# A decoder layer on one core: the down projection as seven products of halves, with the sums of weights made by adding DMAs

## The chip, the core and the metric

The kernel runs on one core of a Trainium2 chip. The metric is the device time of one execution in microseconds (us). TensorE is called PE here (its weight loads PEld), VectorE DVE, ScalarE ACT, GpSimd POOL, and the SyncE queue that issues most DMAs SP.

## What is computed

One layer of a decoder for 512 tokens of width 1024, in float32: token mixers, an output projection, a gated feed-forward part with a causal convolution of width 3, and a last RMS norm. What matters here is the end of it:

```python
x  = x + merged @ w_out[l]                       # (512, 1024)
def conv_gated_ffn(h, w_up, conv_w, conv_b, w_down):
    up = causal_depthwise_conv(h @ w_up, conv_w, conv_b)     # (512, 5632)
    gate, val = jnp.split(up, 2, axis=-1)
    return (jax.nn.silu(gate) * val) @ w_down                # (512, 2816) @ (2816, 1024)
x  = x + conv_gated_ffn(rms_norm(x, ffn_norm[l]), ...)
return rms_norm(x, final_norm)
```

## The kernel before

Everything is float32, and TensorE multiplies a rounded form of it (F32R). To keep the precision each operand is split in two: a cast on ACT gives the high part, a subtraction on DVE the low part (`wsplit` for weights, L65; `split` for activations, L75), and each product is three matmuls, high with high, high with low and low with high (`mm3`, L79). So a weight tile goes through a DMA on SP's queue (`wtile`, three buffers of 128x1024), an ACT cast (L70, three buffers), a DVE subtraction (L71, three buffers) and then PE. The order of the instructions on each engine is drawn up by a scheduler when the program is built: it goes by the order of the program, but lets an instruction pass earlier ones that are not ready yet by its own estimate of times. On the chip each engine then follows its list in order.

The last three stages are those around the change:

- Output projection (L561 to L581): the residual stream x1 is held with features on the partitions, 8 tiles of 128 features x 512 tokens.
- Up stage (L615 to L627): 22 pairs of up projections (gate and value), each 8 x 3 matmuls of 512 columns into one PSUM bank (`up`, L591), then the convolution on DVE and ACT (`conv`, L600), SiLU, the product with the value and a split into aH[i] and aL[i] (L627): 22 blocks of 128 features x 512 tokens.
- Down stage (L642 to L736): out = w_down^T a, features on the partitions. Six blocks of 128 output features take 22 x 3 matmuls of 512 columns each (tiles pd, L648). The last 256 features go by 384 tokens in two banks (pA, L690) and, for the last 128 tokens, with tokens on the partitions (pB, L706), so that the norm of these is short. For that, x1 of the last tokens is transposed on PE in the middle (L694), means are taken on PE (L695, L712) and spread (L714).

The tail is everything behind the last matmul: a square with its sum on ACT (L727), two small steps on DVE and POOL for the inverse root (L729, L731), the scaling (L732 to L734) and two output DMAs (L735, L736).

## Time and profile before

| | |
|---|---|
| median of 3 runs | 707.83 us (707.31 to 708.87) |
| the profiled execution's own time | 707.67 us |
| its span on the core | 705.8 us |
| PE busy | 698.0 us (99%) |
| DVE busy | 476.1 us (67%) |
| ACT busy | 332.4 us (47%) |
| POOL busy | 12.3 us (2%) |
| DMA | 69.63 MB, mean 99 GB/s |

Busy time is that of one execution. Matmuls are pipelined: a row's duration (389 ns for 512 columns) is longer than the distance from one start to the next, and it is the distance that counts. The profiled execution lies 0.16 us under the median.

### The profile page before, as it was taken

How to read it: one execution, taken by the hardware profiler on the slowest of the kernel's cores; microseconds unless marked ns; L12 is line 12 of the kernel's file. 1: busy time of each engine (PE TensorE's matmuls, PEld its weight loads, DVE VectorE, ACT ScalarE, POOL GpSimd, SP SyncE). 2: the span in 40 equal slices, each digit the busy share in tenths (PEclk: the TensorE clock that was granted, in tenths of full speed). 3: DMA queues.
4: the chain of work that ended last, by engine and by line, in shares of the span. 5: the costliest groups of instructions: out<-in, count | busy, mean ns of one | idle time of the engine just before them, and what ended most of it. 6: DMA issues, size and time to landing. Idle time of an engine off the chain costs nothing.

```text
span 705.8 us, 8631 instructions
## 1 busy us (share of the span) xinstructions
PE 698.0 (99%) x3303; PEld 587.1 (83%) x3303; DVE 476.1 (67%) x817; ACT 332.4 (47%) x497; POOL 12.3 (2%) x16
## 2 busy tenths in 40 slices
PE   9999999999999999999999999999999999999996
PEld 6888888888888888888888888888888888888896
DVE  7976799877777578755587777777777775433104
ACT  5465566676667533433464444444444444423101
POOL 0000110000000000000100000000000000000000
PEclk9999999999999999999999999999999999999998
DMA  8524422131211122533222232223222335631003
GB/s 255 184 71 143 168 83 82 60 113 47 70 64 61 39 81 80 188 99 111 90 90 91 92 115 91 91 92 115 92 90 91 104 90 164 193 89 47 0 1 120
DMA packets 22617, 69.63 MB, mean 99 GB/s; under 512 B 2736, under 2 KB 4400, under 8 KB 22576
## 3 DMA queue, kind: packets, MB, share of 16 engines
q1 hardware_dynamic: 21568, 66.72, 29.0%
q10 hardware_dynamic: 1008, 2.36, 0.9%
q8 instruction: 26, 0.43, 0.2%
q14 instruction: 15, 0.12, 0.1%
HBM read 66.97 MB, written 2.10 MB: 98 GB/s over the span
## 4 chain that ended last, share of the span: by engine, by line
PE 97%; DMA 1%; DVE 1%; SPq 0%; issue 0%; POOLq 0%; ACT 0%; DVEq 0%
PE pup L82 11%; PE pup L81 11%; PE pup L80 11%; PE pd L81 4%; PE pd L82 4%; PE pd L80 4%; PE pout L81 2%; PE pv L80 2%; PE pout L80 2%; PE pza L80 2%; PE pzb L80 2%; PE pza L81 2%; PE pzu L81 2%; PE pzb L82 2%; PE pzb L81 2%; PE pza L82 2%
## 5 line engine op out<-in xcount | busy, mean ns | idle before, releaser
L70 ACT CAST wh_u<-wr_u 128x1024 fp32r<-128x1024 f32 x44 | 46.3, 1052 | 41.3 <-PE pup L81 29.5
L71 DVE TENSOR_TENSOR wl_u<-wr_u,wh_u 128x1024 fp32r<-128x1024 f32 x44 | 53.9, 1226 | 8.0 <-ACT wh_u L70 7.0
L605 DVE TENSOR_TENSOR z<-pup,r 128x512 f32<-128x512 f32 x44 | 30.2, 688 | 35.2 <-PE pup L82 35.2
L80 PE MATMUL pd<-aH,wh_d 128*128 128x512 f32 x132 | 51.3, 389 | 0.0
L81 PE MATMUL pd<-aL,wh_d 128*128 128x512 f32 x132 | 51.3, 389 | 0.0
L82 PE MATMUL pd<-aH,wl_d 128*128 128x512 f32 x132 | 51.3, 389 | 0.0
L70 ACT CAST wh_g<-wr_g 128x1024 fp32r<-128x1024 f32 x24 | 25.2, 1049 | 46.2 <-issue 27.4
L76 ACT CAST aH<-y 128x512 fp32r<-128x512 f32 x22 | 13.7, 621 | 56.8 <-DVE z L604 54.2
L71 DVE TENSOR_TENSOR wl_d<-wr_d,wh_d 128x896 fp32r<-128x896 f32 (+1 forms) x18 | 20.5, 1136 | 29.0 <-ACT wh_d L70 27.6
L70 ACT CAST wh_d<-wr_d 128x896 fp32r<-128x896 f32 (+1 forms) x18 | 17.7, 982 | 43.0 <-PE pd L81 35.4
L607 ACT ACTIVATE y<-z,part 128x512 f32<-128x512 f32 x44 | 35.9, 818 | 3.1 <-DVE z L605 1.8
L71 DVE TENSOR_TENSOR wl_g<-wr_g,wh_g 128x1024 fp32r<-128x1024 f32 x24 | 29.4, 1223 | 7.0 <-ACT wh_g L70 6.9
L611 DVE SCALAR_TENSOR_TENSOR y<-z,part,y 128x512 f32<-128x512 f32 x44 | 33.0, 751 | 1.4
L609 DVE SCALAR_TENSOR_TENSOR y<-z,part,y 128x512 f32<-128x512 f32 x44 | 32.8, 747 | 0.3 <-ACT y L607 0.3
L624 ACT ACTIVATE y<-y 128x512 f32<-128x512 f32 x22 | 13.9, 632 | 36.6 <-DVE y L611 36.6
L80 PEld LDWEIGHTS pd<-aH,wh_d 128*128 128x128 f32 x132 | 24.8, 188 | 5.2
L81 PEld LDWEIGHTS pd<-aL,wh_d 128*128 128x128 f32 x132 | 24.8, 188 | 5.1
L82 PEld LDWEIGHTS pd<-aH,wl_d 128*128 128x128 f32 x132 | 24.8, 188 | 5.1
L81 PE MATMUL pout<-mL,wh_o 128*128 128x512 f32 x64 | 25.3, 395 | 0.0
L80 PE MATMUL pout<-mH,wh_o 128*128 128x512 f32 x64 | 25.0, 394 | 0.0
L82 PE MATMUL pout<-mH,wl_o 128*128 128x512 f32 x64 | 24.9, 389 | 0.0
L77 DVE TENSOR_TENSOR aL<-y,aH 128x512 fp32r<-128x512 f32 x22 | 15.2, 693 | 14.2 <-ACT aH L76 14.2
(595 smaller groups left out, 2004.8 us busy)
## 6 DMA issues: line engine op xcount, KB each, us to landing
wr_u<-in_w_u_dram SPq DMA_DIRECT2D x44, 512.0 KB, 3.3
wr_g<-in_w_g_dram SPq DMA_DIRECT2D x24, 512.0 KB, 3.3
wr_d<-in_w_d_dram SPq DMA_DIRECT2D x12, 448.0 KB, 3.5
x<-in_xT_dram SPq DMA_DIRECT2D x16, 256.0 KB, 4.2
wr_v<-in_w_v_dram SPq DMA_DIRECT2D x8, 512.0 KB, 4.3
wr_o<-in_w_o_dram SPq DMA_DIRECT2D x8, 512.0 KB, 3.3
wr_d<-in_w_d_dram SPq DMA_DIRECT2D x6, 512.0 KB, 3.5
wr_e<-in_w_e_dram SPq DMA_DIRECT2D x5, 512.0 KB, 3.8
```

Of the source, the lines that this page charges most:

```text
L70: A.copy(th[:, lo:hi], raw[:, lo:hi])
L71: V.tensor_tensor(out=tl[:, lo:hi], in0=raw[:, lo:hi], in1=th[:, lo:hi].bitcast(F32), op=ALU.subtract)
L76: A.copy(th, src)
L77: V.tensor_tensor(out=tl, in0=src, in1=th.bitcast(F32), op=ALU.subtract)
L80: T.matmul(o, lhsT=wh, rhs=xh, start=start, stop=False)
L81: T.matmul(o, lhsT=wh, rhs=xl, start=False, stop=False)
L82: T.matmul(o, lhsT=wl, rhs=xh, start=False, stop=stop)
L605: V.tensor_tensor(out=z[:, 2:], in0=pz, in1=r2, op=ALU.mult)
L607: A.activation(out=y, in_=z[:, 2:], func=AF.Identity, scale=part[:, w + 2:w + 3], bias=part[:, PCB + f:PCB + f + 1])
L609: V.scalar_tensor_tensor(out=y, in0=z[:, 1:S + 1], scalar=part[:, w + 1:w + 2], in1=y, op0=ALU.mult, op1=ALU.add)
L611: V.scalar_tensor_tensor(out=y, in0=z[:, 0:S], scalar=part[:, w:w + 1], in1=y, op0=ALU.mult, op1=ALU.add)
L624: A.activation(out=yg, in_=yg, func=AF.Silu)
```

## The change

The down projection is computed with tokens on the partitions, as a product of 2 x 2 halves: the tokens (A1, A2) and the 2816 inner features in halves on one side, the inner features and the 1024 output features in halves (B11, B12, B21, B22) on the other. Seven products of halves, m1, m5, m6, m4, m3, m7 and m2 in this order, take the place of eight. Each is 256 tokens x 1408 x 512 features: 11 inner blocks x 2 blocks of tokens x 3 matmuls of 512 columns, in six steps (two inner blocks each, one in the last) with one weight tile per step.

- The activations' sides: `up` no longer splits its result, but writes it to aT; every fourth pair `a_sides` makes the sums and differences of halves on DVE, and splits that of m1. The sides of the other six are split in the down stage (`a_split`, three blocks of up to 128x1024 per product, two steps ahead).
- The weights' sides: six tiles R hold B11, loaded on SP's queue in the up stage (pairs 12 to 17). After a tile has been split for one product (`w_split`, two steps ahead), the next half is added into it by a DMA from GpSimd's queue with an adding form (`fill` with `accum_op`): B12 after m1, B22 after m5, B21 after m6, B12 after m3, 24 adding DMAs in all. After m4, B22 is loaded plainly on SP's queue; m2 loads B21 through the tiles wr.
- The residual x1 is turned to tokens on the partitions in the up stage (`x1_turn`, eight times four PE transposes and one ACT copy), and added on DVE. The results of the products are added into it on DVE as they come (`post`); the norm is taken per token (`done`, `finish`), and each block of 128 tokens leaves by one DMA on SP's queue and one on ACT's.
- The last product runs its last three steps for one block of tokens and then for the other.
- gfb, the final gain on all partitions, is loaded on ACT's queue at the start of the down stage instead of on SP's at the start of the kernel. The layouts of w_u, w_d and the output follow; w_e is gone.

```diff
@@ -161,8 +160,8 @@
     hL = [None] * KC
 
     def htiles(j, n):
-        hH[j] = hp.tile([P, S], F32R, tag=f"hH{j}", name=f"hH{j}{n}")
-        hL[j] = hp.tile([P, S], F32R, tag=f"hL{j}", name=f"hL{j}{n}")
+        t = hp.tile([P, D], F32R, tag=f"h{j}", name=f"h{j}{n}")
+        hH[j], hL[j] = t[:, :S], t[:, S:]
...
-    vA = [hp.tile([P, D], F32, tag=f"d{t}", name=f"vA{t}") for t in range(NT)]
+    vA2 = [hp.tile([P, 2 * D], F32, tag=f"d{t}", name=f"vA{t}") for t in range(2)]
+    vA = [vA2[t // 2][:, (t % 2) * D:(t % 2 + 1) * D] for t in range(NT)]
...
-        SY.dma_start(gfb, fnl.to_broadcast([P, 2 * P]))
...
-        x1t = [hp.tile([P, D], F32, tag=f"d{t}", name=f"x1_{t}") for t in range(NT)]
-        x1 = [x1t[j // 2][:, (j % 2) * S:(j % 2 + 1) * S] for j in range(KC)]
+        x1t = [hp.tile([P, NT, NT, P], F32, tag=f"d{t}", name=f"x1_{t}") for t in range(2)]
+        x1 = [x1t[j // NT][:, j % NT].rearrange("p t c -> p (t c)") for j in range(KC)]
...
-    f2 = ctx.enter_context(tc.tile_pool(name="f2", bufs=2))
     r2 = fp.tile([P, S], F32, name="r2")
-    aH = [fp.tile([P, S], F32R, name=f"aH{i}") for i in range(NF)]
-    aL = [fp.tile([P, S], F32R, name=f"aL{i}") for i in range(NF)]
+    aT = fp.tile([P, NF, S], F32, name="aT")
+    KH = NF // 2
+    S2 = S // 2
+    s1 = fp.tile([P, KH, S2], F32, name="s1")
+    s4 = fp.tile([P, KH, S2], F32, name="s4")
+    a1h = fp.tile([P, KH, S2], F32R, name="a1h")
+    a1l = fp.tile([P, KH, S2], F32R, name="a1l")
+    steps = [(g, min(g + 2, KH)) for g in range(0, KH, 2)]
+    NS = len(steps)
+    B11, B12, B21, B22 = (w_d[k, f] for k in range(2) for f in range(2))
+    R = [fp.tile([P, (hi - lo) * S], F32, name=f"r1_{lo}") for lo, hi in steps]
+    def cols(g):
+        lo, hi = steps[g]
+        return slice(lo * S, hi * S)
+    def fill(q, g, add=True):
+        if add:
+            G.dma_start(R[g], q[:, cols(g)], accum_op=ALU.add)
+        else:
+            SY.dma_start(R[g], q[:, cols(g)])
+    def a_sides(lo, hi):
+        A11, A21 = aT[:, lo:hi, :S2], aT[:, lo:hi, S2:]
+        A12, A22 = aT[:, KH + lo:KH + hi, :S2], aT[:, KH + lo:KH + hi, S2:]
+        h_, l_, s1_, s4_ = (t[:, lo:hi] for t in (a1h, a1l, s1, s4))
+        split(h_, l_, A11)
+        V.tensor_tensor(out=s1_, in0=A21, in1=A22, op=ALU.subtract)
+        V.tensor_tensor(out=A21, in0=A11, in1=A21, op=ALU.subtract)
+        V.tensor_tensor(out=A11, in0=s1_, in1=A11, op=ALU.subtract)
+        V.tensor_tensor(out=s4_, in0=A12, in1=A11, op=ALU.add)
...
-    for i in range(NF):
-        pg = up(2 * i)
...
-        V.tensor_tensor(out=yv, in0=yg, in1=yv, op=ALU.mult)
-        split(aH[i], aL[i], yv)
...
-    for j in range(KC - 2):
-        pd = bank(f"pd{j}")
...
-    pB = bank("pB")
...
+    def x1_turn(t, hf):
+        pt = bank(f"pt{t}{hf}")
+        for q in range(NT):
+            T.transpose(pt[:, q * P:(q + 1) * P], x1t[hf][:, q, t, :], ident)
+        A.copy(x1t[hf][:, :, t, :], pt.rearrange("p (q c) -> p q c", q=NT))
+    with tc.tile_pool(name="f2", bufs=2) as f2:
+        for n in range(NF):
+            i = n // 2 + (n % 2) * KH
+            pg = up(2 * n)
+            if n == 0:
+                rt = rooted([acc2], 0, f2, "f")
+                pv = up(1)
+                A.copy(r2, over_partitions(rt, f2, "f"))
+            yg = conv(pg, i)
+            if n:
+                pv = up(2 * n + 1)
+            A.activation(out=yg, in_=yg, func=AF.Silu)
+            yv = conv(pv, NF + i)
+            V.tensor_tensor(out=aT[:, i], in0=yg, in1=yv, op=ALU.mult)
+            if n % 4 == 3 or n == NF - 1:
+                a_sides(n // 4 * 2, n // 2 + 1)
+            if 4 <= n < 12:
+                x1_turn((n - 4) // 2, n % 2)
+            if 12 <= n < 12 + NS:
+                fill(B11, n - 12, False)
+    dp = ctx.enter_context(tc.tile_pool(name="dp", bufs=1))
+    blocks = [(0, 4), (4, 8), (8, KH)]
+    ms = dp.tile([P, NT, 4], F32, name="ms")
+    gfb = dp.tile([P, D], F32, name="gfb")
+    A.dma_start(gfb, fnl.to_broadcast([P, D]))
+    left = {
+        "m5": lambda lo, hi: s1[:, lo:hi],
+        "m6": lambda lo, hi: aT[:, lo:hi, :S2],
+        "m4": lambda lo, hi: aT[:, KH + lo:KH + hi, S2:],
+        "m3": lambda lo, hi: s4[:, lo:hi],
+        "m7": lambda lo, hi: aT[:, lo:hi, S2:],
+        "m2": lambda lo, hi: aT[:, KH + lo:KH + hi, :S2],
+    }
+    order = ["m1", "m5", "m6", "m4", "m3", "m7", "m2"]
+    after = {"m1": (B12, True), "m5": (B22, True), "m6": (B21, True), "m4": (B22, False), "m3": (B12, True)}
+    parts = {}
+    def a_split(n, b):
+        lo, hi = blocks[b]
+        w = (hi - lo) * S2
+        ah = hp.tile([P, D], F32R, tag=f"h{b}", name=f"ah_{n}{lo}")
+        al = hp.tile([P, D], F32R, tag=f"h{3 + b}", name=f"al_{n}{lo}")
+        split(ah[:, :w].rearrange("p (k t) -> p k t", t=S2), al[:, :w].rearrange("p (k t) -> p k t", t=S2),
+              left[n](lo, hi))
+        parts[n, b] = (ah, al)
+    def a_of(n, k, m):
+        if n == "m1":
+            return tuple(t[:, k, m * P:(m + 1) * P] for t in (a1h, a1l))
+        c = slice((k % 4) * S2 + m * P, (k % 4) * S2 + (m + 1) * P)
+        return tuple(t[:, c] for t in parts[n, k // 4])
+    ws_ = {}
+    def w_split(n, g):
+        c = cols(g)
+        w = c.stop - c.start
+        raw = wtile(B21[:, c], f"{n}{g}", cols=w) if n == "m2" else R[g]
+        ws_[n, g] = wsplit(raw, f"{n}{g}", 0, w)
+        if n in after:
+            fill(after[n][0], g, after[n][1])
+    def res(t, f):
+        return x1t[f][:, :, t, :]
+    def b3(t):
+        return t.rearrange("p (q c) -> p q c", q=NT)
+    def plus(t, f, t_):
+        V.tensor_tensor(out=res(t, f), in0=res(t, f), in1=b3(t_), op=ALU.add)
+    def done(t, f, p_, op=ALU.add):
+        V.tensor_tensor(out=res(t, f), in0=res(t, f), in1=b3(p_), op=op)
+        j_ = dp.tile([P, S], F32, tag="j", name=f"j{t}{f}", bufs=2)
+        A.activation(out=b3(j_), in_=res(t, f), func=AF.Square, accum_out=ms[:, t, f:f + 1])
+        if f:
+            V.tensor_tensor(out=res(t, f), in0=res(t, f), in1=b3(gfb[:, S:]), op=ALU.mult)
+    def finish(t):
+        V.tensor_scalar(out=ms[:, t, 2:3], in0=ms[:, t, 0:1], scalar1=ms[:, t, 1:2], scalar2=1.0 / D,
+                        op0=ALU.add, op1=ALU.mult)
+        V.tensor_scalar(out=ms[:, t, 2:3], in0=ms[:, t, 2:3], scalar1=EPS, scalar2=None, op0=ALU.add)
+        G.tensor_tensor(out=ms[:, t, 3:4], in0=ms[:, t, 2:3], in1=mhalf[:, 0:1], op=ALU.pow)
+        r_ = ms[:, t, 3:4]
+        V.scalar_tensor_tensor(out=res(t, 0), in0=res(t, 0), scalar=r_, in1=b3(gfb[:, :S]),
+                               op0=ALU.mult, op1=ALU.mult)
+        A.mul(res(t, 1), res(t, 1), r_)
+        SY.dma_start(out[t, :, :S], res(t, 0))
+        A.dma_start(out[t, :, S:], res(t, 1))
+    p1, p5 = ([dp.tile([P, S], F32, name=f"{n}{m}") for m in range(2)] for n in ("p1", "p5"))
+    def post(n, b, ms_=(0, 1)):
+        for m in ms_:
+            if n == "m1":
+                A.copy(p1[m], b[m])
+                plus(m, 0, p1[m])
+            if n == "m5":
+                A.copy(p5[m], b[m])
+            if n == "m6":
+                V.tensor_tensor(out=p1[m], in0=b[m], in1=p1[m], op=ALU.add)
+                V.tensor_tensor(out=p5[m], in0=p5[m], in1=p1[m], op=ALU.subtract)
+                plus(m, 1, p5[m])
+                plus(2 + m, 1, p5[m])
+            if n == "m4":
+                V.tensor_tensor(out=p1[m], in0=b[m], in1=p1[m], op=ALU.add)
+                plus(2 + m, 0, p1[m])
+            if n == "m3":
+                done(m, 1, b[m])
+            if n == "m7":
+                done(2 + m, 0, b[m])
+                done(2 + m, 1, b[m], ALU.subtract)
+                finish(2 + m)
+            if n == "m2":
+                with tc.high_priority():
+                    done(m, 0, b[m])
+                    finish(m)
+    seq = [(n, g) for n in order for g in range(NS)]
+    turn_ = {}
+    for i, n in enumerate(order[1:], 1):
+        for b in range(3):
+            turn_.setdefault(b if i == 1 else NS * (i - 1) + (4, 6, 8)[b], []).append((n, b))
+    for g in range(2):
+        w_split(*seq[g])
+    acc_ = None
+    def steps_of(n, g, ms_):
+        wh, wl = ws_[n, g]
+        lo, hi = steps[g]
+        for k in range(lo, hi):
+            cw = slice((k - lo) * S, (k - lo + 1) * S)
+            for m in ms_:
+                ah, al = a_of(n, k, m)
+                mm3(acc_[m], ah, al, wh[:, cw], wl[:, cw], k == 0, k == KH - 1)
+    for i, (n, g) in enumerate(seq):
+        if i + 2 < len(seq):
+            w_split(*seq[i + 2])
+        for x in turn_.get(i, ()):
+            a_split(*x)
+        if g == 0:
+            acc_ = [bank(f"{n}_{m}") for m in range(2)]
+        if n != order[-1] or g < NS - 3:
+            steps_of(n, g, (0, 1))
+            if g == NS - 1:
+                post(n, acc_)
+    for m in range(2):
+        for g in range(NS - 3, NS):
+            steps_of(order[-1], g, (m,))
+        post(order[-1], acc_, (m,))
```

## Rows read from the trace of the kernel before

**Rows 1.** page, part 1 (busy time), part 4 (chain that ended last)

```profile
PE 698.0 (99%) x3303; PEld 587.1 (83%) x3303; DVE 476.1 (67%) x817; ACT 332.4 (47%) x497; POOL 12.3 (2%) x16
...
PE 97%; DMA 1%; DVE 1%; SPq 0%; issue 0%; POOLq 0%; ACT 0%; DVEq 0%
```

**Rows 2.** stretches: length, busy and count per engine, PE clock, DMA, GB/s

```profile
335.60:576.40 240.80, 240.80 (x1068) 199.54 (x1067) 175.66 (x265) 110.56 (x139) 1.85 (x1) 1.00 0.29 96
576.40:666.10 89.70, 89.70 (x397) 74.30 (x396) 34.51 (x44) 30.08 (x42) 0.00 (x0) 1.00 0.34 102
666.10:689.90 23.80, 23.80 (x141) 23.75 (x140) 2.66 (x5) 2.50 (x4) 0.00 (x0) 1.00 0.00 1
689.90:699.40 9.50, 9.50 (x79) 9.32 (x78) 5.38 (x13) 2.13 (x5) 0.86 (x1) 1.00 0.15 52
```

**Rows 3.** timeline of PE (start, us, what): first pd, first pA

```profile
576.35 0.39 PE L80 MATMUL pd<-aH,wh_d 128*128 128x512 f32 x1
...
666.11 0.33 PE L80 MATMUL pA<-aH,eH 128*128 128x384 f32 x1
```

**Rows 4.** timeline of PE around the six transposes of before

```profile
672.20 0.34 PE L82 MATMUL pA<-aH,eL 128*128 128x384 f32 x1
672.38 0.60 PE L694 MATMUL pTa<-cstt,x 128*128 128x128 f32 x4
...
673.03 0.28 PE L121 MATMUL pm_B<-mcol,acc 128*128 128x1 f32 x2
673.17 0.42 PE L80 MATMUL pA<-aH,eH 128*128 128x384 f32 x1
673.43 0.34 PE L81 MATMUL pA<-aL,eH 128*128 128x384 f32 x1
```

**Rows 5.** timeline of DVE at the end of the up stage

```profile
565.67 0.69 DVE L605 TENSOR_TENSOR z<-pup,r 128x512 f32<-128x512 f32 x1 [1.73 <-PE pup L82]
566.57 1.23 DVE L71 TENSOR_TENSOR wl_d<-wr_d,wh_d 128x1024 fp32r<-128x1024 f32 x1 [0.21 <-ACT wh_d L70]
567.71 0.75 DVE L609 SCALAR_TENSOR_TENSOR y<-z,part,y 128x512 f32<-128x512 f32 x1
```

**Rows 6.** groups of DVE, 335 to 706 us: busy, mean ns

```profile
L611 DVE SCALAR_TENSOR_TENSOR y<-z,part,y 128x512 f32<-128x512 f32 x44 | 33.0, 751 | 1.4
...
L77 DVE TENSOR_TENSOR aL<-y,aH 128x512 fp32r<-128x512 f32 x22 | 15.2, 693 | 14.2 <-ACT aH L76 14.2
```

**Rows 7.** the same of ACT, with idle time before and releasers

```profile
L70 ACT CAST wh_d<-wr_d 128x1024 fp32r<-128x1024 f32 x6 | 6.3, 1054 | 11.4 <-PE pd L81 9.1 <-DMA wr_d<-in_w_d_dram 1.3 <-PE pup L81 1.0
...
L652 ACT ACTIVATE sq<-x 128x512 f32<-128x512 f32 x5 | 3.2, 634 | 14.2 <-DVE x L650 14.2
```

**Rows 8.** timeline of the tail, all engines

```profile
699.14 0.28 PE L82 MATMUL pB<-xh,aL 128*128 128x256 f32 x1
699.46 0.38 ACT L727 ACTIVATE oB<-pB 128x256 f32<-128x256 f32 x1 [4.45 <-PE pB L82]
...
699.97 0.42 DVE L728 TENSOR_TENSOR xB<-pB,gfb 128x256 f32<-128x256 f32 x1 [0.39 <-ACT oB L727]
700.31 0.20 DVE L729 TENSOR_SCALAR mB<-mB 128x1 f32<-128x1 f32 x1
...
700.73 0.55 POOL L731 TENSOR_TENSOR mB<-mB,mhalf 128x1 f32<-128x1 f32 x1 [6.74 <-DMA out_dram<-x]
...
702.21 0.33 SPq L736 DMA_DIRECT2D out_dram<-oB  x1
```

**Rows 9.** DMA: queue (packets, MB, share); issues (count, KB, us landing)

```profile
q1 hardware_dynamic: 21568, 66.72, 29.0%
...
wr_u<-in_w_u_dram SPq DMA_DIRECT2D x44, 512.0 KB, 3.3
...
bsb<-in_bs_dram ACTq DMA_DIRECT2D x1, 512.0 KB, 7.7
```

**Rows 10.** groups of POOL

```profile
L148 POOL TENSOR_TENSOR rt_f<-ms_f,mhalf 128x4 f32<-128x4 f32 x1 | 1.9, 1855 | 225.6 <-DVE ms_f L147 225.6
```

More of the change, by code (lines that the diff above doesn't have):

```diff
@@ L43, in block_kernel @@
 def block_kernel(ctx, tc, xT, pos, w_s, w_v, w_g, w_q, w_kv, w_o, w_u, w_d,
-                 ws_t, bs, vg, vb, par, cst, w_e, fnl, out, outB):
+                 ws_t, bs, vg, vb, par, cst, fnl, out):
     nc = tc.nc
@@ L86, in block_kernel @@
     gx = cp.tile([P, KC], F32, name="gx")
-    gfb = cp.tile([P, 2 * P], F32, name="gfb")
     cstt = cp.tile([P, NCST], F32, name="cstt")
@@ L683, in block_kernel @@
-    n = S - P
-    tA, tB = slice(0, n), slice(n, S)
-    pA, sqA = None, []
-    for j in (KC - 2, KC - 1):
-        pA = bank(f"pA{j}")
-        for i in range(NF):
-            c = slice((j - KC + 2) * P, (j - KC + 3) * P)
-            mm3(pA[:, :n], eh[i][:, c], el[i][:, c], aH[i][:, tA], aL[i][:, tA], i == 0, i == NF - 1)
-            if j == KC - 2 and i == 11:
-                pT = [bank("pTa"), bank("pTb")]
-                for k in range(KC - 2):
-                    T.transpose(pT[k // 4][:, (k % 4) * P:(k % 4 + 1) * P], x1[k][:, tB], ident)
-                pmB = bank("pm_B")
-                col_mean(pmB[:, :1], [acc3[:, tB]], 0)
-                mB = fp.tile([P, 4], F32, name="mB")
-                V.tensor_scalar(out=mB[:, 0:1], in0=pmB[:, 0:1], scalar1=EPS, scalar2=None, op0=ALU.add)
-        V.tensor_tensor(out=x1[j][:, tA], in0=pA[:, :n], in1=x1[j][:, tA], op=ALU.add)
-        sq = f2.tile([P, n], F32, tag="z", name=f"sqA{j}")
-        A.activation(out=sq, in_=x1[j][:, tA], func=AF.Square)
-        V.tensor_tensor(out=acc3[:, tA], in0=acc3[:, tA], in1=sq, op=ALU.add)
-        A.mul(x1[j][:, tA], x1[j][:, tA], gain(j))
@@ L704, in block_kernel @@
-    pB = bank("pB")
-    for i in range(NF):
-        mm3(pB[:, :256], aH[i][:, tB], aL[i][:, tB], eh[i], el[i], i == 0, i == NF - 1)
-        if i == 1:
-            for k in range(2):
-                T.matmul(pB[:, k * P:(k + 1) * P], lhsT=x1[KC - 2 + k][:, tB], rhs=ident, start=False, stop=False)
-        if i == 4:
-            rt = rooted([acc3[:, tA]], 0, f2, "A", cols=NT - 1)
-        if i == 12:
-            pb = over_partitions(rt, f2, "A", cols=NT - 1)
-            for q in range(KC // 2):
-                for j in (2 * q, 2 * q + 1):
-                    V.tensor_tensor(out=x1[j][:, tA], in0=x1[j][:, tA], in1=pb, op=ALU.mult)
-                    if q in (0, 3):
-                        SY.dma_start(out[j], x1[j][:, tA])
-                if q in (0, 3):
-                    continue
-                SY.dma_start(out[2 * q:2 * q + 2].rearrange("j p t -> p j t"),
-                             x1t[q].rearrange("p (j t) -> p j t", j=2)[:, :, tA])
@@ L792 @@
 _ORDER = ["xT", "pos", "w_s", "w_v", "w_g", "w_q", "w_kv", "w_o", "w_u", "w_d", "ws_t", "bs",
-          "vg", "vb", "par", "cst", "w_e", "fnl"]
+          "vg", "vb", "par", "cst", "fnl"]
 def kernel(**inputs):
@@ L813 @@
     r = run_bass_kernel_spmd(nc, [maps], core_ids=[0])
-    a, b = (np.asarray(r.results[0][f"out_{i}_dram"]) for i in range(2))
-    return np.ascontiguousarray(np.concatenate([a.reshape(D, S - P).T, b]))[None]
+    return np.ascontiguousarray(np.asarray(r.results[0]["out_0_dram"]).reshape(S, D))[None]
```

78 lines of the change are left out of this document (5 added, 73 removed).

## The prediction, made before the changed kernel was run

> **What bounds the kernel now.** I read the page's busy times and its chain first: PE is busy 99% of the span and 97% of the chain that ended last is PE [rows 1], so time is won only by fewer PE cycles, as long as nobody makes PE wait. The table of stretches shows where the change works. In the up stage (240.8 us) DVE is busy 175.66 us and ACT 110.56, in the first six blocks of the down stage (89.7 us) DVE only 34.51, and the clock is full in all of them [rows 2]. The down stage lasts from the first pd matmul to the end of pB, 89.70 + 23.80 + 9.50 = 123.0 us [rows 2]. The distance of its matmuls follows from two starts: 396 matmuls of 512 columns between 576.35 and 666.11 [rows 3], 0.2267 us each. DMA is far from full: the transfers of SP's queue took 29.0% of the 16 engines' span [rows 9].
>
> **Products.** Seven products of 11 x 2 x 3 matmuls are 462 of 512 columns, at 0.2267 us 104.7 us (14.96 us a product, 2.72 a full step, 1.36 the last). They replace the 123.0 us, in which the transposes, means and the spread for the norms also lie. Gain 18.3 us. Nothing in the operands is new to PE: the v projection (L292) already has activations stationary and 512 columns of weights moving.
>
> **Turning the residual.** The 32 transposes go to PE in the up stage, where nothing hides them. Before's six take 672.38 to 673.03, 0.108 each, and the first matmul behind such a group takes 0.26 until the next instead of 0.18 [rows 4]. Eight groups of (4 x 0.108 + 0.09) cost 4.2 us. Their copies on ACT (some 0.6 us each, as the 128x512 squares [rows 7]) lie in ACT's 130 idle us of the stage.
>
> **The activations' sides.** The up stage loses 22 subtractions of 128x512 on DVE (15.2 us [rows 6]) and gains five passes over 11 x 256 columns, 14080 columns or 27.5 such tiles, 19 us. The 4 us more are hidden by DVE's 65 idle us there; without that cover they would cost 4. SP's queue gets six loads more in this stage (512 KB land in 3.3 us [rows 9]), at a DMA share of 0.29 [rows 2]: nothing. gfb moves from SP's start, ahead of post and cst, to ACT's queue at the border of the stages, where it must wait until the up stage's buffers are free; behind it on ACT stand the casts of m1, whose first two steps are cast already. PE has 5.4 us of work then, the convolution's tail on DVE is about that long: 0 to 1.5 us, and I take 0.
>
> **DVE in the down stage.** Here is the first cost on the path. Back to back a 128x1024 subtraction starts the next after 1.14 us (566.57 to 567.71 [rows 5]), 0.09 less than its duration, so I take 0.62 for 128x512 (0.693 less the overlap [rows 6]). A product needs 5 x 1.14 + 0.62 = 6.3 us for its weights, 3.2 for the next activations, together 9.5 of 14.96, and then its own `post`: 0 (m5) to 2.5 us for most, but eight passes or 5.0 us behind m6, and 5.7 behind m7 (twice three passes, a fused one of 0.75 and two small steps). ACT has 8.8 us and less than 3 besides, so it isn't the bound. The cast for a step waits for the matmul that frees one of three buffers, as wh_d waited for pd [rows 7]. So the tile of step 2 of the next product can't be split before the last matmul of this one. PE needs it 5.44 us later, and in the program `post` stands ahead of it: a leftover of 0.8 plus 5.0 plus 1.14 is 6.9 us behind m6, 7.6 behind m7. In strict order that is 1.4 and 2.1 us of waiting PE, together 3.5. But the rows show a split of weights put between two steps of a convolution, 9.8 us ahead of its matmul [rows 3, 5], so the list is mixed, and the lower end is 0. Others that could wait add a little. I take 2.0, and 0 to 5 for the range.
>
> **Adding DMAs.** Each waits in POOL's queue for both readers of its tile; POOL has 12.3 us of work in all [rows 1], and behind the adds stand only the roots of m7 and m2, which come after the last of them. The casts of the next product wait for the sum, and with them everything behind them on ACT. No row shows an adding DMA. Three waves follow each other (behind m1, m5 and m6), 3 x 5.5 full tiles of 512 KB. They can begin some 4.5 us ahead of m1 (the first down tile of before was split 8.5 us ahead [rows 3, 5], the next are held by the buffers), and the last sum is wanted before the last step of m4, 3 x 14.96 + 5 x 2.72 - 2.4 = 56.1 us behind m1's start. With 3 us for issue and landing, PE waits 16.5 c - 57.6 us, where c is the time of one full add on the engines: nothing up to c = 3.5. A plain load takes 66.72 MB / (0.29 x 16 x 705.8 us) = 20.4 GB/s per engine, so c = 1.6; that is the lower end. If the tile is read as well, the engines move twice as much: c = 3.2. The upper end is the slowest transfer of this size, 7.7 us to landing [rows 9]: 69 us of waiting, and 15 more in the fourth wave (behind m3). I take 3.2, since a second read of the same bytes is what the addition must do: 0 us. What is late next is then DVE's list, counted above. The plain loads behind m4 and those of m2 go on SP's queue, where nothing else waits but the outputs: 0.
>
> The Trainium skill (Collectives: The Full Stack, section on the bandwidth ceiling) says that a reducing transfer is held up not by its addition but by its two source reads on one ring, and runs at about half the rate of a copy. By that c would be 3.2 as well and the sum would not change; no run here has shown it yet.
>
> **Tail.** Before: from the last matmul's start (699.14) a square of 256 columns at 699.46, the product with gfb, the small step at 700.31, POOL at 700.73, and the last output issue at 702.21 [rows 8]. After: an addition of 0.69 first, a square of 512 columns (0.63 for 0.38 [rows 7, 8]), no product with gfb in between (-0.35), one small step more (0.2), the fused scaling of 0.75 as long as what it replaces. 0.69 + 0.05 + 0.25 - 0.35 + 0.2 = 0.8 us more; the outputs have the same size. With one hand-over less or more 0.4 to 1.4.
>
> **Sum.** -18.3 + 4.2 + 2.0 + 0 + 0.8 = -11.3 us. The profiled execution, 707.67 us with a span of 705.8, becomes 707.67 - 11.3 = 696.4 us, its span 694.5. It lies 0.16 us below the median, which I leave out. Within these terms, 693 (no waiting, a short tail) to 700.
>
> **Rivals.** (1) The adds are late, the one that ends on the other side. Its place is the first matmuls of each step of m5, m6 and m4, its price 16.5 c - 57.6: it decides from c = 3.5, eats the whole gain at c = 4.2, and c = 5, three times a plain load, gives 696.4 + 24.9 = 721.3 us. For it: no row shows such a transfer, and the margin between 3.2 and 4.2 is thin. Against it: DMA is two thirds idle [rows 2]. Slower through this: 0.17; late by less than the gain: 0.07 (697 to 706).
>
> (2) DVE's list becomes the bound. It has some 86 us of work (7 x 6.3 + 6 x 3.2 + 23 of `post`) in 104.7, where before it had 42.6 in 123.0 [rows 2]. If waits of 1.4 to 2.1 us come at all six borders of products instead of two, 8.4 to 12.6 us in place of 2.0, the time is 702.8 to 707.0. Against it: four of the six have a `post` of at most 2.5 us. Chance 0.12, of which 0.02 end above 706.4.
>
> (3) The issue on POOL binds. Its slowest plain step took 1.9 us [rows 10]; 18 issues of that are 34 us and hidden. At 4 us each, 72 - 57.6 = 14 us of waiting, 710.8 us. The Trainium skill (SBUF — State Buffer, Summary: rules for kernel authors) advises against hiding a transfer issued from GpSimd under DVE, because descriptor generation starves while DVE is in a fast mode; the same page counts tensor_tensor, which nearly all of DVE's work here is, among those without that mode. Chance 0.05, of which 0.04 slower.
>
> (4) The change doesn't bring what it says: the matmuls are fewer by count, so only a larger distance per matmul could undo that, by 0.024 us each for the whole gain. The weight loads (0.19 us) fit under 0.2267 in the same way as now. Chance 0.01.
>
> **How the numbers follow.** The forecast has the rest, 0.58. Times within 0.2% of before (706.4 to 709.2) are about what a measurement here can't tell from no change. Faster: 0.58 + 0.07 + 0.10 = 0.75; within 0.2%: 0.02 of (2), 0.01 of (3) and (4)'s 0.01 = 0.04; slower: 0.17 + 0.04 = 0.21. The range starts at 692, a us under the best of the terms, and reaches into rival 1 to c = 4.5, 16.7 us late: 713. Left out are the slower part of rival 1, some 0.14, and a few hundredths below 692.
>
> **What would show it.** Right: starts 0.2267 us apart in the products; 14.96 us from bank to bank; adds that land 3 us and more before the cast that reads the tile; PE idle only at step 2 of m4 and m2, 1 to 2 us each. Wrong: casts in m5, m6 and m4 that wait for a DMA (rival 1) or for a POOL issue (rival 3); weight subtractions late behind `post` at every border (rival 2); up stage longer by much more than 4.2 us; a tail over 7.5 us.

## The result, and the profile after

The kernel after takes 696.7 us (median of four runs, 696.55 to 697.01) where the kernel before takes 707.88 (707.31 to 708.87) beside it: a ratio of 0.9841, 95% interval 0.9824 to 0.9858. The forecast was 696.4 us. The profiled execution took 697.01 us and has a span of 695.3 us, where 694.5 were forecast.

The page of after: busy times, the two large DMA queues, and the adding DMAs among the issues (count, size, us from issue to landing).

```profile
PE 684.6 (98%) x3183; PEld 569.4 (82%) x3183; DVE 522.6 (75%) x859; ACT 353.9 (51%) x519; POOL 36.0 (5%) x42
...
q1 hardware_dynamic: 21408, 62.92, 27.4%
q0 software_dynamic: 3456, 11.54, 9.3%
...
wr_u<-in_w_u_dram SPq DMA_DIRECT2D x44, 512.0 KB, 3.3
...
r<-in_w_d_dram POOLq DMA_DIRECT2D x20, 512.0 KB, 7.2
```

The stretches of after: up stage, seven products, tail. Columns: length, then busy time and count of PE, PEld, DVE, ACT, POOL, then PE's granted clock (1.00 is the full 2.4 GHz), the busy share of the 16 DMA engines, GB/s.

```profile
335.90:580.75 244.85, 244.85 (x1101) 202.72 (x1100) 181.01 (x272) 104.40 (x133) 3.79 (x3) 1.00 0.33 105
580.75:686.40 105.65, 105.07 (x463) 86.39 (x461) 82.90 (x99) 61.57 (x79) 22.26 (x25) 1.00 0.75 158
686.40:695.30 8.90, 0.14 (x1) 0.00 (x0) 2.46 (x5) 2.16 (x4) 0.55 (x1) 0.69 0.43 119
```

PE is busy 13.4 us less than before [rows 1], the span 10.5 us shorter. These 10.5 us fall apart by stages as follows. The first matmul of `up` in before, and in after the first of `up` and of m1:

```profile
335.56 0.39 PE L80 MATMUL pup<-hH0f,wh_u 128*128 128x512 f32 x1
```

```profile
336.05 0.39 PE L80 MATMUL pup<-h0f,wh_u 128*128 128x512 f32 x1
...
580.75 0.39 PE L80 MATMUL m<-wh_m,a1h 128*128 128x512 f32 x1
```

From the first matmul of `up` to the first of m1 the up stage takes 244.70 us, where before took 240.79, to 576.35 [rows 3]: +3.9. The products take 105.6 us in place of 123.0: -17.4. From the last matmul's start (686.15) to the end of the span it is 9.15 us, before 6.66: +2.5. The first `up` began 0.5 us later than before's; in the other kernels below, which are the same up to there, it began anywhere from 335.23 to 336.39 us, so this is no part of the change. -17.4 + 3.9 + 2.5 + 0.5 = -10.5 us, the difference of the spans.

PE waits for another engine only once in the products. The timeline of PE in m2:

```profile
680.97 0.39 PE L82 MATMUL m<-wh_m,al_m 128*128 128x512 f32 x1
681.94 0.50 PE L82 MATMUL m<-wh_m,al_m 128*128 128x512 f32 x1 [0.58 <-DVE al_m L77]
682.27 0.39 PE L80 MATMUL m<-wh_m,ah_m 128*128 128x512 f32 x1
```

From the first row to the second it is 0.74 us more than the usual 0.23, from the second to the third 0.10 more. What DVE and POOL did before it:

```profile
678.61 1.22 DVE L71 TENSOR_TENSOR wl_m<-wr_m,wh_m 128x1024 fp32r<-128x1024 f32 x1
...
678.77 1.46 POOL L741 TENSOR_TENSOR ms<-ms,mhalf 128x1 f32<-128x1 f32 x1 [2.18 <-DVE ms L740]
...
680.27 0.75 DVE L743 SCALAR_TENSOR_TENSOR x<-x,ms,gfb 128x512 f32<-128x512 f32 x1 [0.44 <-POOL ms L741]
...
680.93 0.95 DVE L77 TENSOR_TENSOR al_m<-aT,ah_m 128x768 fp32r<-128x768 f32 x1
```

The split of the last activations (al_m) stands behind the scaling of a block that is already finished, and that scaling waits for the root on POOL. The root itself took 1.46 us: it began beside the 128x1024 subtraction on DVE and ended 0.40 us behind that one's end (679.83). In the tail, with DVE idle, the same step takes 0.54 to 0.55 us, and 0.54 where the fastest version below puts it into idle time of DVE. At that length it would have been done at 679.3, and DVE would not have stood idle for 0.44 us; this is an estimate, and no run changes that alone.

At step 2 of m4 and of m2, where the prediction put the waits, PE doesn't wait. The weight subtraction for step 2 of m4, and the matmul that reads it, at the usual distance from the one before:

```profile
629.89 1.22 DVE L71 TENSOR_TENSOR wl_m<-r,wh_m 128x1024 fp32r<-128x1024 f32 x1
...
631.07 0.39 PE L80 MATMUL m<-wh_m,ah_m 128*128 128x512 f32 x1
...
631.29 0.39 PE L81 MATMUL m<-wl_m,ah_m 128*128 128x512 f32 x1
```

The tail of after, all engines:

```profile
686.15 0.39 PE L82 MATMUL m<-wh_m,al_m 128*128 128x512 f32 x1
686.39 0.72 ACT L745 ACTIVATE x<-x,ms 128x512 f32<-128x512 f32 x1 [1.09 <-POOL ms L741]
686.39 0.75 DVE L743 SCALAR_TENSOR_TENSOR x<-x,ms,gfb 128x512 f32<-128x512 f32 x1 [0.66 <-POOL ms L741]
687.06 0.68 DVE L730 TENSOR_TENSOR x<-x,m 128x512 f32<-128x512 f32 x1
...
687.78 0.63 ACT L732 ACTIVATE j<-x 128x512 f32<-128x512 f32 x1 [0.66 <-DVE x L730]
...
689.01 0.55 POOL L741 TENSOR_TENSOR ms<-ms,mhalf 128x1 f32<-128x1 f32 x1 [2.65 <-DVE ms L740]
...
690.34 0.47 ACTq L747 DMA_DIRECT2D out_dram<-x  x1
```

The last addition (687.06) is ready to go when PE is done, but stands behind the scaling of the block before it (L743). From the last matmul's start to the last issue it is 4.19 us, before 3.07 [rows 8]; from there to the end 4.96, before 3.59.

### The profile page after: what moved, and what is told of

It is laid out like the page before. It is cut to its first block, busy times and chain, and to the rows that moved or that the text cites. A ratio compares the mean times of both kernels' runs of the same rounds, so it can differ in the third digit from the quotient of the medians.

```text
span 695.3 us, 8489 instructions
## 1 busy us (share of the span) xinstructions
PE 684.6 (98%) x3183; PEld 569.4 (82%) x3183; DVE 522.6 (75%) x859; ACT 353.9 (51%) x519; POOL 36.0 (5%) x42
## 3 DMA queue, kind: packets, MB, share of 16 engines
q1 hardware_dynamic: 21408, 62.92, 27.4%
q0 software_dynamic: 3456, 11.54, 9.3%
## 4 chain that ended last, share of the span: by engine, by line
PE 96%; DVE 1%; issue 1%; POOL 0%; ACT 0%; POOLq 0%
PE pup L80 12%; PE pup L82 12%; PE pup L81 11%; PE m L82 4%; PE m L81 4%; PE m L80 4%; PE pout L81 2%; PE pv L80 2%; PE pout L80 2%; PE pza L81 2%; PE pza L80 2%; PE pzb L80 2%; PE pzb L82 2%; PE pzu L81 2%; PE pzb L81 2%; PE pv L82 2%
## 5 line engine op out<-in xcount | busy, mean ns | idle before, releaser
L82 PE MATMUL m<-wh_m,al_m 128*128 128x512 f32 x132 | 51.5, 390 | 0.6 <-DVE al_m L77 0.6
L80 PE MATMUL m<-wh_m,ah_m 128*128 128x512 f32 x132 | 51.4, 389 | 0.0
L81 PE MATMUL m<-wl_m,ah_m 128*128 128x512 f32 x132 | 51.4, 389 | 0.0
L71 DVE TENSOR_TENSOR wl_m<-r,wh_m 128x1024 fp32r<-128x1024 f32 (+1 forms) x36 | 40.7, 1131 | 6.3 <-ACT wh_m L70 6.3
L70 ACT CAST wh_m<-r 128x1024 fp32r<-128x1024 f32 (+1 forms) x36 | 35.3, 980 | 19.6 <-PE m L82 19.1
L606 POOL DMA_DIRECT2D r<-in_w_d_dram x24 | 21.4, 890 | 287.0 <-DVE wl_m L71 270.7
L639 DVE SCALAR_TENSOR_TENSOR y<-z,part,y 128x512 f32<-128x512 f32 x44 | 32.8, 747 | 0.7 <-ACT y L637 0.7
L82 PEld LDWEIGHTS m<-wh_m,al_m 128*128 128x128 f32 x132 | 24.8, 188 | 6.1 <-DVE al_m L77 1.0
L81 PEld LDWEIGHTS m<-wl_m,ah_m 128*128 128x128 f32 x132 | 24.8, 188 | 5.2
L80 PEld LDWEIGHTS m<-wh_m,ah_m 128*128 128x128 f32 x132 | 24.8, 188 | 5.2
L77 DVE TENSOR_TENSOR al_m<-aT,ah_m 128x1024 fp32r<-128x1024 f32 (+1 forms) x12 | 13.6, 1134 | 11.9 <-ACT ah_m L76 11.9
```

The source lines that it names most:

```text
L70: A.copy(th[:, lo:hi], raw[:, lo:hi])
L71: V.tensor_tensor(out=tl[:, lo:hi], in0=raw[:, lo:hi], in1=th[:, lo:hi].bitcast(F32), op=ALU.subtract)
L77: V.tensor_tensor(out=tl, in0=src, in1=th.bitcast(F32), op=ALU.subtract)
L80: T.matmul(o, lhsT=wh, rhs=xh, start=start, stop=False)
L81: T.matmul(o, lhsT=wh, rhs=xl, start=False, stop=False)
L82: T.matmul(o, lhsT=wl, rhs=xh, start=False, stop=stop)
```

## Experiments

My theory after the result: the adds are hidden; 3.9 us are PE's own time for turning the residual; what remains against the sum lies in one wait in m2 and in the tail. The rivals were that the adds cost something that can't be seen, that the up stage is longer for another reason, and that the end is late for a fixed reason. A time without a range is that of one run; the kernel before lay between 707.31 and 710.14 us in all its runs beside these, so differences of a us or two between such times mean little.

### Are the adds hidden? The sums replaced by plain loads

```diff
-            G.dma_start(R[g], q[:, cols(g)], accum_op=ALU.add)
+            SY.dma_start(R[g], q[:, cols(g)])
```

> Leaves the sums of the weights out: the 24 adding transfers from GpSimd's queue become plain loads on SP's queue into the same tiles, behind the same readers; everything else is as in the changed kernel. My theory: the adds are hidden, so the time stays at 696.4 to 697.0 us (ratio to before 0.984) and the wait of PE at the last product (0.7 to 0.9 us, behind DVE's list) stays. Rival: the adds already hold the casts back or crowd the DMA engines; then 1 us or more is won, 695.7 or less.

Measured: 696.64 us (696.4 to 697.25), ratio 0.9839 (0.9819 to 0.9858), and the same wait in m2 (0.75 + 0.10 us). The adds cost nothing that can be seen here.

The room is small, though. In after's third wave (behind m6, for m4) the sums land 2.3 to 4.9 us ahead of the casts that read them. The closest of them, its issue and its cast:

```profile
617.90 0.88 POOL L606 DMA_DIRECT2D r<-in_w_d_dram  x1 [1.62 <-issue]
```

```profile
628.54 1.06 ACT L70 CAST wh_m<-r 128x1024 fp32r<-128x1024 f32 x1 [1.16 <-PE m L82]
```

This sum landed 8.3 us after its issue, at 626.2, and the cast waited for PE, not for it.

### How much more would they bear? Two kernels with second adds

```diff
+            G.dma_start(R[g], q[:, cols(g)], accum_op=ALU.add)
```

and, in the other kernel, on the first half of the columns alone:

```diff
+            c = cols(g)
+            w = (c.stop - c.start) // 2
+            G.dma_start(R[g][:, :w], q[:, c.start:c.start + w], accum_op=ALU.add)
```

> Every adding transfer is made twice, so the sums are other than wanted and the engines' time for one full tile doubles. The changed kernel's trace gives that time as 2.5 us by the distance of POOL's issues in the busy stretch and 2.9 us by the queue's share, so it becomes 5.0 or 5.9 us. My theory (nothing up to 3.5 us, then 16.5 c - 57.6): 25 us more by the first, 40 by the second: 722 to 737 us, casts waiting for the adds in m5, m6 and m4. Rival, that the adds have much more room than I counted: less than 10 us more.

> Every adding transfer is followed by a second one over the first half of its columns (the sums are other than wanted), so one tile costs 1.5 times as much: 3.75 us by the distance of the issues, 4.4 by the queue's share. My theory: 16.5 c - 57.6 gives 4 us more by the first and 15 by the second: 701 to 712 us. Rival, more room: within 1 us of the changed kernel, 697.7 or less.

Measured: 750.1 us (+53) and 733.8 us (+37), more than the formula of the prediction, 16.5 c - 57.6, had given. Of this 46 and 32 us lie in m5, m6 and m4, for which it was made (25 to 40 and 4 to 15 were expected); m7, behind the fourth wave, which it leaves out, became 8.0 and 5.3 us longer. Two waits of the half version (total, times, longest):

```profile
POOL r L609 <- DMA r<-in_w_d_dram: 70.3, 24, 6.7
ACT wh_m L70 <- DMA r<-in_w_d_dram: 51.5, 17, 6.8
```

A second add into the same tile has to wait for the landing of the first, and holds POOL's queue while it waits, so POOL's queue now also waits out landings, 24 of them. Neither run doubles the bytes alone. They show three things nonetheless. The rival is real: with late sums PE stands at the casts. Its price is more than the waits themselves, since PE then also ran at a lower granted clock: 0.77 as the mean from 610.7 to 625.7 us in the half version (columns as above):

```profile
610.70:625.70 15.00, 9.70 (x31) 6.82 (x32) 4.12 (x4) 3.64 (x5) 5.31 (x6) 0.77 1.01 171
```

And two stretches say what an add takes on the engines as long as adds are alone, of after and then of the doubled version:

```profile
595.70:610.70 15.00, 15.00 (x68) 12.42 (x67) 10.24 (x11) 8.70 (x11) 5.35 (x7) 1.00 1.05 193
```

```profile
595.70:610.70 15.00, 10.59 (x37) 7.79 (x37) 5.39 (x6) 3.92 (x5) 6.20 (x7) 0.89 1.00 183
```

With nearly nothing but adds, the 16 engines are busy all the time (1.00) at 183 GB/s, so 0.524 MB take 2.87 us; by products (m5, m6, m4) it is 30.4, 29.5 and 30.7 us for 11 full adds, 2.7 to 2.8 us each. After's own waves run at 193 GB/s with a share of 1.05: that is one add per 2.72 us, the pace of the products. The share alone doesn't show that the engines can carry no more: the crowded runs below carry 243 to 278 GB/s at 1.06.

### The sums on DVE instead

```diff
-            G.dma_start(R[g], q[:, cols(g)], accum_op=ALU.add)
+            c = cols(g)
+            w = c.stop - c.start
+            raw = wtile(q[:, c], f"s{len(ws_)}", cols=w)
+            V.tensor_tensor(out=R[g], in0=R[g], in1=raw[:, :w], op=ALU.add)
```

> The sums of the weights are made on DVE: each half is loaded plainly on SP's queue into a tile wr and added into R by a DVE addition, 20 of 128x1024 and 4 of 128x512 more. DVE's 82.9 us of work in the down stage of 105.65 become 82.9 + 20 x 1.14 + 4 x 0.62 = 108. My theory: DVE's list becomes the bound and its order makes PE wait at the borders: 6 to 15 us more, 703 to 712 us. Rival, that DVE has room and the adding transfers aren't needed: within 1 us of the changed kernel.

Measured: 704.1 us, +7.4 against after. The products' stretch is 113.1 us with DVE at 105.28:

```profile
580.90:694.00 113.10, 109.09 (x464) 86.90 (x462) 105.28 (x121) 61.33 (x77) 2.72 (x3) 0.98 0.48 149
```

So against sums on DVE the adding DMAs are worth 7.4 us of this change. With them on DVE its list becomes the bound, much as rival 2 had it: of the six longest waits of PE five end with a subtraction on DVE and one with a cast on ACT.

### Room beside the adds: useless loads, first in one tile, then in three

```diff
+            c = cols(g)
+            dm = dp.tile([P, 1024], F32, tag="dm", name=f"dm{len(ws_)}", bufs=1)
+            SY.dma_start(dm[:, :c.stop - c.start], q[:, c])
```

These lines stand beside each add.

> The kernel after with a useless plain load of the same bytes beside each adding DMA (on SP's queue, into a tile that nobody reads). It takes time on the 16 engines without lengthening the chain from one add to the next. An add takes 2.5 us (spacing of the issues) to 2.9 us (the queue's share) on the engines, a plain load 1.6: together c is 4.1 to 4.5. By my formula 16.5 c - 57.6, PE waits 10 to 17 us: 707 to 714 us. Rival: the engines have room, since the landing of an add (7.2 us) and not its bytes sets its pace: under 1 us more, 697.7 us or less. Between the two: the loads are queued on SP ahead of m2's weights and delay only these.

Measured: 729.5 us, and for another reason than either theory. No wait of PE over 0.3 us until 639.57, in m5, m6 and m4, though the engines carried 243 GB/s from 595.3 to 625.3 where after carries 185 to 193:

```profile
595.30:610.30 15.00, 15.00 (x67) 12.40 (x67) 10.24 (x11) 8.70 (x11) 5.29 (x6) 1.00 1.06 243
```

Then PE waited 18 us at the first step of m3:

```profile
639.57 0.39 PE L82 MATMUL m<-wh_m,al_m 128*128 128x512 f32 x1
657.85 0.79 PE L80 MATMUL m<-wh_m,ah_m 128*128 128x512 f32 x1 [17.89 <-ACT wh_m L70]
```

The loads went one after the other, 13 of them in 66 us, and the plain loads of B22 for m3 stood behind them on SP's queue:

```profile
585.97 66.11 SPq L609 DMA_DIRECT2D dm<-in_w_d_dram  x13
652.18 0.85 SPq L611 DMA_DIRECT2D r<-in_w_d_dram  x2
```

That run says what a transfer off the path costs on the wrong queue, 32.8 us, and leaves the room beside the adds open. So I took three tiles and the first three waves alone:

```diff
+            n_ = len(ws_)
+            if n_ <= 3 * NS:
+                c = cols(g)
+                if n_ % 3 == 1:
+                    dm = dp.tile([P, D], F32, tag="dm", name=f"dm{n_}", bufs=1)
+                else:
+                    dm = hp.tile([P, D], F32, tag=f"h{6 + n_ % 3 // 2}", name=f"dm{n_}")
+                SY.dma_start(dm[:, :c.stop - c.start], q[:, c])
```

> Again useless plain loads of the same bytes beside the adding DMAs, but only for the three waves behind m1, m5 and m6 (18 loads), into three tiles that nobody reads, so that they don't hold up SP's queue one behind the other: before, they went one at a time, 5.1 us each, still ran at 652 us and kept the plain loads of m3 waiting (18 us of PE there), while PE didn't wait in m5, m6 and m4. Theory now: the engines have room for 17 full loads of 1.6 us beside the three waves, and the lead of the sums over their casts (3 us and more after landing) swallows the rest: no wait of PE over 0.5 us in m5, m6 and m4, the kernel's time within 1.5 us of after, 695.2 to 698.2 us. Rival, my formula: 27 us of engine time more in the three waves, with c = 2.5 to 2.7 for an add 16.5 c - 57.6 + 27 = 11 to 14 us of waiting PE, at the first matmuls of the steps of m5, m6 and m4: 707 to 711 us.

Measured: 706.0 us, +9.3. The theory fell; the formula, with 11 to 14 us, was nearer and too high. Up to 618 us PE doesn't wait; then it loses 1.00, 0.88, 1.99, 1.03, 0.73 and 1.27 us at the first matmuls of steps, in m6 and m4, and 1.26 at the border to m3, together 8.2; the rest of the 9.3 us are the 0.1 us behind each of these and smaller waits. The casts there, in the timeline of ACT:

```profile
613.37 1.05 ACT L70 CAST wh_m<-r 128x1024 fp32r<-128x1024 f32 x1 [1.23 <-DMA r<-in_w_d_dram]
617.22 1.05 ACT L70 CAST wh_m<-r 128x1024 fp32r<-128x1024 f32 x1 [2.06 <-DMA r<-in_w_d_dram]
621.00 1.05 ACT L70 CAST wh_m<-r 128x1024 fp32r<-128x1024 f32 x1 [1.79 <-DMA r<-in_w_d_dram]
...
628.24 1.04 ACT L70 CAST wh_m<-r 128x1024 fp32r<-128x1024 f32 x1 [3.03 <-DMA r<-in_w_d_dram]
```

This is rival 1 as it would have looked. A stretch of it on the engines:

```profile
610.50:625.50 15.00, 13.52 (x57) 10.30 (x57) 7.86 (x8) 8.04 (x10) 4.22 (x5) 1.00 1.06 278
```

Of POOL's issues, 10.5 full adds lie between 596.64 and 635.46, 3.70 us each with their share of the loads, and an add lands after 9.9 us (median) instead of 7.2. My 57.6 us had 3 us for issue and landing in it; with 9.9 it is 50.7, and 16.5 x 3.70 - 50.7 = 10.4 us, for 8.2 measured. This fit was made after the run, with its own numbers.

### What lengthened the up stage? No turning of the residual

```diff
-            if 4 <= n < 12:
-                x1_turn((n - 4) // 2, n % 2)
```

> The kernel after without the turning of the residual: the 32 transposes on PE and their eight copies on ACT are left out (the residual stays with features on the partitions, so the output is another one). My term for them is 4.2 us of PE time that nothing hides, and the up stage of after was 3.9 us longer than before's. If that is so: 3.9 to 4.2 us less than after, 692.5 to 692.8 us, and an up stage of 240.5 to 241.0 us from the first matmul of up to the first of m1. Rival: the 3.9 us come from the DVE work added to the stage (the sides, +4 us on DVE) or from the loads of B11 and the larger gaps at PSUM banks: then under 1 us less, 695.7 us or more.

Measured: 692.83 us (692.32 to 693.59), ratio 0.9788 (0.9775 to 0.9801). The first `up` and the first m1:

```profile
335.54 0.39 PE L80 MATMUL pup<-h0f,wh_u 128*128 128x512 f32 x1
...
576.37 0.39 PE L80 MATMUL m<-wh_m,a1h 128*128 128x512 f32 x1
```

That is within 0.1 us of before's 240.79. All of the 3.9 us are the transposes with their copies. The five passes on DVE (180.12 us busy in that stage), the loads of B11 and the moved gfb cost nothing.

### Is it only the product fewer? By token with eight products

All sums are taken out, and the activations are split in the up stage as before; eight plain products of halves follow, in the order of `seq`:

```diff
-            V.tensor_tensor(out=aT[:, i], in0=yg, in1=yv, op=ALU.mult)
-            if n % 4 == 3 or n == NF - 1:
-                a_sides(n // 4 * 2, n // 2 + 1)
+            V.tensor_tensor(out=yv, in0=yg, in1=yv, op=ALU.mult)
+            split(aH[i], aL[i], yv)
...
+    seq = [(f, k, g) for f in (1, 0) for k in range(2) for g in range(NS)]
```

> By token as in after, with the residual turned and added on DVE, but with eight plain products of halves instead of seven: no sums of weights or activations, no adding DMAs. Theory: the whole gain is one product fewer. 528 matmuls of 512 columns at 0.2267 us are 119.7 us instead of 105.6, so +14.1 us, 710.8 us: slower than before by 3 us, since turning the residual (+3.9) and the longer tail (+2.5) cost more than the transposes and means of the norms that go (-3.3). Rival: the form by token itself brings part of the gain: 705 us or less. Other rival: DVE waits at the borders of products were part of after's stage: then less than +14.

Measured: 709.27 us, +12.6, and by this one run not to be told from the kernel before (708.0 beside it, 707.46 to 709.47). PE never waits in the products: they end at 699.8, 119.7 us after 580.09, which is +14.1 as expected. Its tail is 1.2 us shorter than after's (7.96 us from the last matmul's start). So the form by token brings nothing by itself that this run could show; the gain is the eighth product.

### The tail: whole rows, and the order on DVE

With each output written by the scaling into a whole tile (o0 and o1, the tiles p1 and p5, free by then), a row that leaves is 2 KB instead of four pieces of 512 bytes:

```diff
-        SY.dma_start(out[t, :, :S], res(t, 0))
-        A.dma_start(out[t, :, S:], res(t, 1))
...
+        SY.dma_start(out[t, :, :S], o0)
+        A.dma_start(out[t, :, S:], o1)
```

> The kernel after with its eight outputs written by the scaling into whole tiles of 512 columns, so that a row that leaves is 2 KB instead of four pieces of 512 bytes. Theory: 1.4 us of the tail (4.96 us from the last issue to the end, 3.59 before) are the price of the 512-byte pieces. Then -0.5 to -1.4 us, 695.3 to 696.2 us, with 3.6 to 4.2 us from the last issue to the end. Rival: the end is late for another reason (four transfers in a short time on the same engines, or a fixed cost behind the last one): the same time within 0.2 us, and 4.8 to 5.0 us from the last issue to the end.

Measured: 695.55 us (695.37 to 697.43; ratio 0.9832, 0.9819 to 0.9845), and 3.93 us from the last issue to the end. That is -1.15 in the median, but I don't credit the rows with all of it: ten kernels with 512-byte pieces show 4.24 to 4.97 us there, in two groups (4.2 to 4.4 and 4.9 to 5.0), and the two kernels further below, with whole rows for the last two blocks, 4.25 and 4.22. The means are 4.65 and 4.13: about half a us. The difference lies in the landing of the last output on ACT's queue: 3.2 to 3.3 us behind its issue in five kernels and 3.8 to 3.9 in the other five, after among them, against 2.8 with whole rows (where in two of the three kernels the output on SP's queue lands later, at 3.2). In every kernel 1.0 to 1.2 us follow the last landing. Why the pieces land at two distances stays open.

The other edit puts the last block's addition ahead of the scaling of the block before it (`finish` is split into `root` and `scale` for this):

```diff
-                    done(m, 0, b[m])
-                    finish(m)
+                    add = done(m, 0, b[m])
+                    if m:
+                        with tc.issue_after(getattr(add, "ins", add)):
+                            scale(0)
+                    root(m)
+                    if m:
+                        scale(m)
```

> The kernel after with one change in DVE's list at the very end: the last addition of the last block of tokens goes ahead of the scaling of the block before it. Theory: the addition waited 0.6 us for that scaling, between the last matmul and the last issue (4.2 us, 3.07 before). Then -0.5 to -0.6 us, 696.1 us, and 3.5 to 3.7 us from the last matmul's start to the last issue. Rival: something behind it (ACT's square, the small steps) is as late anyway: no change in that distance.

Measured: 697.03 us (696.39 to 698.44), and 3.97 us from the last matmul's start to the last issue instead of 4.19. The addition began 0.49 us sooner behind the matmul, but ACT was then late:

```profile
686.28 0.69 DVE L730 TENSOR_TENSOR x<-x,m 128x512 f32<-128x512 f32 x1 [0.85 <-PE m L82]
686.84 0.38 ACTq L750 DMA_DIRECT2D out_dram<-x  x1
...
687.27 0.63 ACT L732 ACTIVATE j<-x 128x512 f32<-128x512 f32 x1 [0.45 <-DVE x L730]
```

The square waits for an output issue of the block before, which is in ACT's list ahead of it. More than half of the expected 0.5 us went there; in the time nothing is seen. The rival was nearer.

### Together

Both edits of the tail (whole rows for the last two blocks only), and in m2:

```diff
-                finish(2 + m)
+                root(2 + m)
...
+            if x == (order[-1], 2):
+                with tc.issue_after(getattr(al, "ins", al)):
+                    scale(2)
+                    scale(3)
```

Here `al` is the subtraction of the last activations.

> The kernel after with three edits: the output rows of the last two blocks whole (2 KB), the last block's addition ahead of the scaling before it, and in m2 the subtraction for the last three inner blocks ahead of the scalings of the first two finished blocks, which there stood behind POOL's root. Theory: the three are independent and stand on the path: -0.5 to -1.4, -0.5 to -0.6 and -0.8 (the one wait of PE in the down stage, 0.75 + 0.10), together -1.8 to -2.8 us, 693.9 to 694.9 us, and no wait of PE over 0.3 us in m2. Rival: the scalings that are put back collide with the end, so that less than 1 us is won.

Measured: 695.81 us (695.45 to 696.06; ratio 0.9829, 0.9815 to 0.9842), so under 1 us was won over after, as the rival said. The wait in m2 had only moved: the two scalings, now behind al_m, stood ahead of the last weight subtraction, and PE waited 0.66 + 0.11 us for that. One edit more puts the scalings behind that subtraction (`low`) as well:

```diff
+            if seq[i + 2] == (order[-1], NS - 1):
+                low = last_low[0]
+                with tc.issue_after(getattr(low, "ins", low)):
+                    scale(2)
+                    scale(3)
```

> As the run before with three edits, but the scalings of the two finished blocks stand on DVE behind the last weight subtraction of m2, not only behind the activations' subtraction: there they delayed that weight subtraction, and PE waited 0.66 + 0.11 us for it instead of 0.75 + 0.10. Theory: DVE is idle 0.8 us ahead of the next addition, so the two scalings (1.4 us) fit there. Then no wait of PE over 0.3 us in m2, last matmul 0.7 us earlier, 694.9 to 695.1 us. Rival: PE waits again for the next thing in DVE's list, and the time is that of the run before, 695.8 us.

Measured: 694.95 us (694.42 to 696.99), ratio 0.9816 (0.9799 to 0.9834): the fastest version that leaves nothing out. DVE around it:

```profile
679.37 0.95 DVE L79 TENSOR_TENSOR al_m<-aT,ah_m 128x768 fp32r<-128x768 f32 x1
680.24 0.69 DVE L73 TENSOR_TENSOR wl_m<-wr_m,wh_m 128x512 fp32r<-128x512 f32 x1
680.84 1.41 DVE L750 SCALAR_TENSOR_TENSOR x<-x,ms,gfb 128x512 f32<-128x512 f32 x2
...
682.29 0.69 DVE L733 TENSOR_TENSOR x<-x,m 128x512 f32<-128x512 f32 x1
```

The scalings fit just ahead of the next addition, PE waits nowhere in the products by more than 0.1 us, and the tail is 3.71 + 4.22 us in place of 4.19 + 4.96. By the medians 1.75 us against after; the intervals of the two ratios overlap, so the step itself rests on the traces.

## Why the prediction held, step by step

- **Products.** 104.7 us and 2.0 of waiting were forecast, 105.6 came. Matmuls start 0.2267 us apart, the products 14.95 us. The version with eight products shows the price of one by itself, 14.1 us with DVE's wait counted in.
- **Turning the residual.** 4.2 forecast, 3.9 measured, and the run without it gives all of that back. The gap behind a group of transposes, 0.09 us, is as [rows 4] showed it.
- **DVE's list.** This term was mis-sized: 2.0 forecast, 0.84 measured, and at another place. At step 2 of m4 and of m2, where I had put 1.4 and 2.1 us in strict order, nothing waits: in m4 the weight subtraction stands between the eight passes of `post` (629.89 us, the next pass at 631.03), and PE reads it at 631.29. That is the mixing that I had taken as the lower end. The real wait, at step 4 of m2, comes from a mechanism that I had not listed, a scaling that waits for POOL's root with a subtraction for PE behind it. (By its own working the 0.62 us for a 128x512 subtraction should have been 0.60, which moves no term.)
- **Adds.** Nothing forecast, nothing measured, but two of the inputs were off, in opposite directions. c is 2.7 to 2.9 us among adds alone, not 3.2, and landing takes 7.2 us (median), not 3. With 7.2 the formula is 16.5 c - 53.4, so waiting begins at c = 3.2, the very value that I took, and the gain is gone at 3.9, not 4.2. The margin was thinner than I wrote; the last crowded run shows it used up. In after's third wave two of the six sums land less than the 3 us ahead of their casts that the prediction named as a sign of being right (2.3 and 2.6).
- **The rule of half the rate.** The queues say the same as the stretches: adds 11.54 MB at 9.3%, 11.2 GB/s per engine; plain loads 62.92 MB at 27.4%, 20.6. An add takes 1.7 to 1.9 times a plain load. The Trainium skill (Collectives: The Full Stack, section on the bandwidth ceiling) puts the reducing phase of a ring collective at about half the rate of the copying one. The trace is near it as long as adds are alone on the engines. Between plain loads an add was cheaper: in the last crowded run a full add and 0.98 of a plain load took 3.70 us, by estimate 2.1 us for the add if the load is put at 1.6.
- **POOL's issues.** The step on POOL took 0.89 us, not the 4 us of rival 3. The Trainium skill (SBUF — State Buffer, Summary: rules for kernel authors) warns of starved descriptor generation on GpSimd under DVE's fast modes. No row here shows it, with DVE busy 82.90 of 105.65 us and the issues at 0.88 to 0.90 us there.
- **Tail.** Mis-sized: +0.8 forecast, +2.5 measured. From the last matmul to the last issue it grew by 1.1 instead of 0.8; the addition began 0.91 us behind the last matmul (0.42 in the fastest version) because of DVE's order, and the other terms were a little high. From the last issue to the end it grew by 1.4, where I had put nothing because the outputs have the same size. They have, but not the same pieces: the last output landed 3.8 us behind its issue, in before 2.5. About 0.5 us goes with the pieces, and the rest stays open: that distance differs by up to 0.7 us between kernels that end alike.

By the medians the total came within 0.3 us, by the profiled spans within 0.8 (695.3 for 694.5), of which 0.5 is the late start of `up` in that execution. So close it came by luck, because misses cancel: DVE's waits 1.2 us and the turning 0.3 below the forecast, the tail 1.7 above it. By the prediction's own signs the tail, 9.15 us for at most 7.5, and the places of PE's waits were wrong. The mechanism of the gain and the large terms were right: one product fewer, the turning unhidden, the adds hidden.
